# A raw-weight ring of six blocks, and four transfers for a paired chunk

## The chip, the core and the metric

The kernel runs on one core of a Trainium2 chip. Five engines work side by side, each through its own queue in order: TensorE (PE, matmuls; PEld is its loading of weights), VectorE (DVE), ScalarE (ACT), GpSimd (POOL) and SyncE (SP, which here only issues transfers). The metric is the device time of one execution in microseconds, lower is better. The profile is one execution taken by the hardware profiler.

## What is computed

One layer of a hybrid block over 512 latent tokens of width 1024, with 256 context tokens. From the normalised and modulated tokens `h`, one wide projection gives ten parts; two branches use them, a gated short convolution and an attention over neighbours, and their outputs are merged and projected.

```python
parts = _split_in(h @ w_in[i])                   # b, c, x, z_a, q, k, v, z_b, g_a, g_b
...
attn = _neighbourhood_attention(q, k, v, k_c, v_c, rpb[i])
...
y_a = (silu(z_a) * b_gate * _dwconv3(c_gate * x_in, conv_w, conv_b)) @ w_out_conv
y_b = (silu(z_b) * attn_o) @ w_out_attn
merged = sigmoid(g_a) * y_a + sigmoid(g_b) * y_b
y = merged @ w_o
x = x + gt[:, None, :] * _rmsnorm(y, post_g[i])
```

All of it is float32. The kernel reaches that precision by splitting every operand into a rounded high part H and a rest L (ACT casts H, DVE subtracts to get L) and multiplying H by H, H by L and L by H.

## The kernel before

**Weights come in chunks.** The host lays `w_in` and the two output projections out as chunks of 1024 rows by 256 columns, 1 MB each: two units of 128 columns side by side, in eight row blocks `k` of 128. `order` (L236 to L240) lists the chunks in the order of their use, and a `Chunks` object hands them out. A `Chunk` (L83) has two raw tiles `raw` of [128, 4, 256], one for the row blocks 0 to 3 and one for 4 to 7, and fills each with a transfer of 512 KB issued on SP (L89). The pool holds three such raw tiles; a fourth can be filled only when the first has no reader left.

**Two kinds of use.** A whole chunk goes through `split` (L91): for each raw tile one ACT cast (L67) and one DVE subtraction (L70) over 1024 elements a partition. A *paired* chunk (`paired`, L233: 20 of the 45) is multiplied by a block scheme with seven block products in place of eight. Its raw tiles are seen as four blocks: B11 and B12 are the two column halves of the first raw tile, B21 and B22 those of the second (L99). `first` (L98) splits B11 and B21 and the sums T1 = B11 + B12 (L102) and T2 = T1 + B22 (L105), adds B22 to B12 (L109) and T2 to B21 (L110), all in place. `second` (L114) splits what is left: T3 in the place of B12, T4 in that of B21, and B22. So the blocks of one raw tile end at different times: B11 with T2, in `first`, and B12 with T3, in `second`.

**Who waits for whom.** Each product runs on PE (`product`, L286; the matmuls are L289), in two halves of `pair` (L294): first B11, B21, T1 and T2, then T4, T3 and B22. L306 and L317 are DVE additions that free a PSUM bank for the next product, L314 further combinations. Between these products stand the attention's steps of the current pair of heads: scores (L721, L730), adding the relative bias and the row maximum on DVE (L737, from a tile `bt` loaded at L713), exponentials on ACT (L744, L748), scaling (L751), transposes on PE (L758), the split of the transposed block into `TH` and `TL` (L67, L70 again), and the product with the values (L777). Loop iterations interleave them by count (`step`, `fill`). While the attention runs, `Chunks.load` defers the first half of the splitting to the end of the iteration by way of the list `behind`.

**What sets the order.** Apart from a hand-written start, a scheduler places the instructions of each engine from their dependences, at build time. After that each engine takes its instructions in that order, and SP its transfers.

Chunk names below: qk*n* (queries and keys of pair *n*), gate chunk *n* (the gates of pairs 2*n* and 2*n*+1 in the attention branch), cx*n* and bz*n* (conv parts), v*n* (values).

Of the kernel before, what the change touches and what calls it, by code (L numbers as in the profile page):

```python
# [9 lines left out]
F32 = mybir.dt.float32  # L10
# [5 lines left out]
P = 128  # L16
D = 1024
KT = 8
S = 512
# [8 lines left out]
def layer(ctx: ExitStack, tc, xp, ctxt, ctxT, cc, wmod, small, wfirst, win, wout, wo, rel, tab, out):  # L28
    nc = tc.nc
# [3 lines left out]
    wp = ctx.enter_context(tc.tile_pool(name="wp", bufs=2))  # L33
# [4 lines left out]
    class Banks:  # L38


        def __init__(self, *tags):
            self.tags, self.n = tags, 0
# [21 lines left out]
    def split(H, L, src, scale=None, pinned=False):  # L64

        if scale is None:
            cast = nc.scalar.copy(H, src)  # L67
            if pinned:
                tc.keep_in_program_order(cast)
            nc.vector.tensor_sub(L, src, H.bitcast(F32))  # L70
        else:
            nc.scalar.mul(H, src, scale)
            nc.vector.scalar_tensor_tensor(
                out=L, in0=src, scalar=scale, in1=H.bitcast(F32), op0=ALU.mult, op1=ALU.subtract
            )
# [4 lines left out]
    def wtile(shape):  # L80
        return wp.tile(shape, F32R, name="w", bufs=4)

    class Chunk:  # L83


        def __init__(self, src):
            self.raws = [wp.tile([P, 4, 256], F32, name="raw", bufs=3) for _ in range(2)]
            for i, raw in enumerate(self.raws):
                nc.sync.dma_start(raw, src[:, 4 * i:4 * i + 4])  # L89

        def split(self):  # L91
            t = [wtile([P, 4, 2, 256]) for _ in range(2)]
            for x, raw in zip(t, self.raws):
                split(x[:, :, 0], x[:, :, 1], raw)
            k = range(KT)
            return tuple([t[i // 4][:, i % 4, y] for i in k] for y in range(2)) + ([t[i // 4][:, i % 4] for i in k],)

        def first(self, keep=False):  # L98
            (b11, b12), (b21, b22) = self.b = [(r[:, :, :P], r[:, :, P:]) for r in self.raws]  # L99
            t, sums = (wtile([P, 2, 2, 4, P]) for _ in range(2))  # L100
            split(t[:, 0, 0], t[:, 0, 1], b11)
            nc.vector.tensor_add(b11, b11, b12)  # L102
            split(sums[:, 0, 0], sums[:, 0, 1], b11)
            split(t[:, 1, 0], t[:, 1, 1], b21)
            nc.vector.tensor_add(b11, b11, b22)  # L105
            split(sums[:, 1, 0], sums[:, 1, 1], b11)
            self.keep = keep
            if not keep:
                nc.vector.tensor_add(b12, b12, b22)  # L109
            nc.vector.tensor_add(b21, b21, b11)  # L110
            self.B = {"B11": t[:, 0], "B21": t[:, 1], "T1": sums[:, 0], "T2": sums[:, 1]}
            return self
# [15 lines left out]
    class Chunks:  # L128
# [4 lines left out]

        def load(self, n):
            if n < len(self.srcs) and n not in self.ahead and n not in self.raw:
                self.raw[n] = Chunk(self.srcs[n][0])
                if behind is None:
                    self.ready(n)
                else:
                    behind.append(lambda: self.ready(n))  # L140
# [153 lines left out]
    def pair(c1, c2, w=None):  # L294

        w = w or chunk().B
        a, b, e = (pj()[:, :256] for _ in range(3))
        first, second = slice(0, 256), slice(256, S)
        product(a, A11, w["B11"], True)
        nc.scalar.copy(c1[:, first], a)  # L300
        product(b, A12, w["B21"], True)
        product(e, blocks_h["X1"], w["T1"], True)
        nc.scalar.copy(c2[:, second], e)
        product(a, blocks_h["S2"], w["T2"], False)
        nc.scalar.copy(c2[:, first], a)
        nc.vector.tensor_add(c1[:, first], c1[:, first], b)  # L306
        chunk.more()
        yield
        product(b, A22, w["T4"], True)
        product(a, blocks_h["S3"], w["T3"], False)  # L310
        nc.scalar.copy(c1[:, second], a)
        product(e, blocks_h["S4"], w["B22"], False)
        for cols, x in ((second, c1[:, second]), (first, e)):
            nc.vector.scalar_tensor_tensor(  # L314
                out=c2[:, cols], in0=c2[:, cols], scalar=-1.0, in1=x, op0=ALU.mult, op1=ALU.subtract
            )
        nc.vector.tensor_add(c1[:, second], c1[:, second], b)  # L317
# [35 lines left out]
    with ExitStack() as p0:  # L353
# [197 lines left out]
        w = chunk()  # L551
# [158 lines left out]
    def scores(p, h, b):  # L710
# [31 lines left out]
        if b % 2 == 0:  # L742
            z = aw.tile([P, 2], F32, name="z", bufs=4)
            nc.scalar.activation(pt, s, AF.Exp, bias=m, scale=-1.0, accum_out=z[:, 0:1])  # L744
            whole[:] = pt, z
        else:
            first, z = whole
            nc.scalar.activation(pt, s, AF.Exp, bias=m, scale=-1.0, accum_out=z[:, 1:2])  # L748
            nc.vector.reciprocal(z, z)  # L749
            for i, x in enumerate((first, pt)):  # L750
                nc.scalar.mul(x, x, z[:, i:i + 1])  # L751
# [96 lines left out]
    blocks = [(p, h, b) for p in range(NPAIR) for h in range(2) for b in range(4)]  # L848
# [54 lines left out]
    us, at = [], []  # L903
# [49 lines left out]
    for j in range(KT):  # L953
        w = chunk()
# [16 lines left out]
        if j == 4:  # L971
# [4 lines left out]
            for i in range(2):  # L976
                gb = cv.tile([P, S], F32, name="ta")
                ps = pj()
                for k in range(4):
                    n = 4 * i + k  # L980
# [3 lines left out]
        if j == 4:  # L984
            A11, S3 = operand("A11", hp, ("u2", "u3")), operand("S3", hp, ("a2", "a3"))
            for q in range(2):
                split(A11[q][:, 0], A11[q][:, 1], raws[q][:, :, h0])
                x = cv.tile([P, S], F32, name="tb").rearrange("p (k c) -> p k c", k=2)
# [219 lines left out]
```

## Time and profile before

| | |
|---|---|
| median of 3 runs | 708.86 us (708.29 to 710.21) |
| the profiled execution | 708.11 us, of which the profile spans 706.3 us |
| TensorE clock granted | 0.998 of full speed |
| DVE busy / ACT busy | 584.9 us / 437.1 us |
| transfers | 108.27 MB, mean 153 GB/s |
| raw halves from `w_in` | 74 transfers of 512 KB, 4.6 us to land (median) |
| raw halves from the output projections | 16 of 512 KB, 3.7 us |
| bias tiles `bt` | 16 of 256 KB, 2.8 us |

Busy time of PE is what the profile models from pipelined matmuls, whose ends lie beyond the next one's start. A bracket behind a row of a timeline is the idle time of that engine just before it and what ended it. In the transfers' rows, SPq is SP's queue, and a row that stands for several issues gives the time from the first to the last.

### The profile page before, as it was taken

How to read it: one execution, taken by the hardware profiler on the slowest of the kernel's cores; microseconds unless marked ns; L12 is line 12 of the kernel's file. 1: busy time of each engine (PE TensorE's matmuls, PEld its weight loads, DVE VectorE, ACT ScalarE, POOL GpSimd, SP SyncE). 2: the span in 40 equal slices, each digit the busy share in tenths (PEclk: the TensorE clock that was granted, in tenths of full speed). 3: DMA queues.
4: the chain of work that ended last, by engine and by line, in shares of the span. 5: the costliest groups of instructions: out<-in, count | busy, mean ns of one | idle time of the engine just before them, and what ended most of it. 6: DMA issues, size and time to landing. Idle time of an engine off the chain costs nothing.

```text
span 706.3 us, 11435 instructions
## 1 busy us (share of the span) xinstructions
PE 694.8 (98%) x4196; PEld 618.4 (88%) x4196; DVE 584.9 (83%) x1114; ACT 437.1 (62%) x868; POOL 67.3 (10%) x111
## 2 busy tenths in 40 slices
PE   7999999999999999999999999999999999999996
PEld 4888888888889989898999999999898899988885
DVE  6989996668599989978899697999799676665996
ACT  7676632556587677775886766878693444442563
POOL 0000003140130310301203103000000000000000
PEclk9999999999999999999999999999999999999999
DMA  9996885565351563552726336313733233570013
GB/s 353 406 344 241 306 329 147 131 170 144 91 109 29 133 177 109 126 137 66 169 101 182 89 122 154 105 61 107 249 115 116 86 120 120 184 264 30 31 59 120
DMA packets 37354, 108.27 MB, mean 153 GB/s; under 512 B 4897, under 2 KB 5153, under 8 KB 37298
## 3 DMA queue, kind: packets, MB, share of 16 engines
q1 hardware_dynamic: 28800, 92.16, 37.8%
q0 software_dynamic: 8352, 15.25, 10.9%
q8 instruction: 33, 0.54, 0.3%
q14 instruction: 23, 0.19, 0.1%
q10 hardware_dynamic: 146, 0.14, 0.1%
HBM read 87.07 MB, written 5.24 MB: 131 GB/s over the span
## 4 chain that ended last, share of the span: by engine, by line
PE 93%; DVE 3%; ACT 2%; DMA 1%; issue 0%; ACTq 0%; DVEq 0%; SPq 0%
PE ps L289 25%; PE ps L164 11%; PE ps L165 11%; PE ps L166 11%; PE ps L177 6%; PE ps L1012 5%; PE ps L777 4%; PE ps L758 4%; PE ps L182 3%; PE ps L721 3%; PE ps L196 2%; PE ps L424 2%; PE ps L430 2%; PE ps L427 2%; PE ps L201 1%; PE ps L730 1%
## 5 line engine op out<-in xcount | busy, mean ns | idle before, releaser
L70 DVE TENSOR_TENSOR w<-raw,w 128x512 fp32r<-128x512 f32 (+1 forms) x193 | 156.2, 823 | 40.0 <-ACT w L67 39.3
L67 ACT CAST w<-raw 128x512 fp32r<-128x512 f32 (+1 forms) x193 | 137.1, 732 | 81.9 <-PE ps L166 28.7
L289 PE MATMUL ps<-S,w 128*128 128x256 f32 x960 | 121.9, 283 | 0.0
L289 PEld LDWEIGHTS ps<-S,w 128*128 128x128 f32 x960 | 118.2, 192 | 0.1
L289 PE MATMUL ps<-h,w 128*128 128x256 f32 x720 | 94.0, 284 | 0.5 <-DVE tc L306 0.4
L289 PEld LDWEIGHTS ps<-h,w 128*128 128x128 f32 x720 | 89.9, 191 | 2.4 <-DVE tc L306 0.7
L164 PE MATMUL ps<-h,w 128*128 128x512 f32 x208 | 81.5, 392 | 0.0
L166 PE MATMUL ps<-h,w 128*128 128x512 f32 x208 | 81.2, 390 | 0.0
L165 PE MATMUL ps<-h,w 128*128 128x512 f32 x208 | 81.0, 389 | 0.0
L630 POOL DMA_DIRECT2D tc<-tb x32 | 28.5, 1165 | 284.1 <-DVE tc L628 197.1
L751 ACT ACTIVATE pt<-pt,z 128x512 f32<-128x512 f32 x64 | 43.0, 722 | 6.1 <-DVE z L749 5.9
L166 PEld LDWEIGHTS ps<-h,w 128*128 128x128 f32 x208 | 39.0, 188 | 8.3
L164 PEld LDWEIGHTS ps<-h,w 128*128 128x128 f32 x208 | 39.1, 188 | 7.9
L165 PEld LDWEIGHTS ps<-h,w 128*128 128x128 f32 x208 | 39.1, 188 | 8.0
L67 ACT CAST TH<-ps 128x512 fp32r<-128x512 f32 x64 | 35.8, 589 | 16.5 <-PE ps L758 16.3
L737 DVE CUSTOM_DVE_ANT_1 ps<-ps,bt 128x512 f32<-128x512 f32 x56 | 38.7, 692 | 7.5 <-PE ps L721 7.2
L70 DVE TENSOR_TENSOR TL<-ps,TH 128x512 fp32r<-128x512 f32 x64 | 42.2, 680 | 0.9 <-ACT TH L67 0.7
L758 PE MATMUL ps<-ident,pt 128*128 128x128 f32 x256 | 33.4, 273 | 0.0
L177 PE MATMUL ps<-w,h 128*128 128x512 f32 x128 | 32.3, 394 | 0.0
L758 PEld LDWEIGHTS ps<-ident,pt 128*128 128x128 f32 x256 | 29.2, 140 | 2.2 <-ACT pt L751 0.2
L744 ACT ACTIVATE pt<-ps,m 128x512 f32<-128x512 f32 x32 | 22.0, 689 | 12.6 <-DVE m L737 11.7
L777 PE MATMUL ps<-TH,V 128*128 128x256 f32 (+1 forms) x96 | 28.5, 319 | 0.2 <-ACT TH L67 0.2
(250 smaller groups left out, 1374.1 us busy)
## 6 DMA issues: line engine op xcount, KB each, us to landing
raw<-in_win SPq DMA_DIRECT2D x74, 512.0 KB, 4.6
wm<-in_wmod SPq DMA_DIRECT2D x34, 512.0 KB, 6.2
raw<-in_wout SPq DMA_DIRECT2D x16, 512.0 KB, 3.7
bt<-in_rel SPq DMA_DIRECT2D x16, 256.0 KB, 2.8
tc<-tb POOLq DMA_DIRECT2D x32, 128.0 KB, 3.4
B<-in_wo SPq DMA_DIRECT2D x8, 512.0 KB, 7.6
fraw<-in_wfirst SPq DMA_DIRECT2D x8, 384.0 KB, 8.3
qd<-qd POOLq DMA_DIRECT2D x24, 128.0 KB, 2.3
```

The costliest lines, as they stand in the source:

```text
L67: cast = nc.scalar.copy(H, src)
L70: nc.vector.tensor_sub(L, src, H.bitcast(F32))
L164: nc.tensor.matmul(ps, lhsT=H[k][:, cs], rhs=mH[k], start=k == 0, stop=False)
L165: nc.tensor.matmul(ps, lhsT=H[k][:, cs], rhs=mL[k], start=False, stop=False)
L166: nc.tensor.matmul(ps, lhsT=L[k][:, cs], rhs=mH[k], start=False, stop=k == KT - 1)
L177: nc.tensor.matmul(ps, lhsT=mH[k][:, ts], rhs=both[k].rearrange("p a c -> p (a c)"), start=k == 0, stop=False, skip_group_check=True,)
L289: nc.tensor.matmul(ps, lhsT=w[:, x, k], rhs=act[y][k], start=start and k + o == 0, stop=k == 3 and o == 2, skip_group_check=True,)
L737: nc.vector.tensor_tensor_reduce(out=s3, in0=s3, in1=bt[:, e::4 - e][:, 0:2], scale=-1.0, scalar=3.0e38, op0=ALU.add, op1=ALU.min, accum_o ...
L751: nc.scalar.mul(x, x, z[:, i:i + 1])
L758: nc.tensor.transpose(tp[:, c], pt[:, c * P:(c + 1) * P], ident)
L777: nc.tensor.matmul(o3[:, dst], lhsT=V[p][:, kt, h], rhs=src(t), start=n == 0 and t is TH, stop=n == len(work) - 1 and t is TL,)
L1012: nc.tensor.matmul(out, lhsT=a(x, k, ts), rhs=w[y][k // 2][:, k % 2, cols], start=start and k + o == 0, stop=k == 3 and o == 2, skip_group ...
```

## The change

The raw tiles give way to one tile, `ring`, of six blocks of 512 elements a partition, as large as the three raw tiles together. A chunk takes two turns of two blocks each, always the next two round the ring. The host now lays every chunk out by blocks: per partition, first the 4 x 128 elements of B11, then those of B12, B21 and B22. A whole chunk still comes in two transfers of 512 KB, now called two blocks each; a paired chunk comes in four of 256 KB, one a block. In `first` the four blocks are the ring's blocks themselves, and so contiguous; in `split` the two blocks of a half are read interleaved (row block, unit, column), so that H and L lie as they did. The number and size of the casts and subtractions is as before.

```diff
+    ring = wp.tile([P, 6, S], F32, name="ring", bufs=1)
+    turn = [0]
...
-        def __init__(self, src):
-            self.raws = [wp.tile([P, 4, 256], F32, name="raw", bufs=3) for _ in range(2)]
-            for i, raw in enumerate(self.raws):
-                nc.sync.dma_start(raw, src[:, 4 * i:4 * i + 4])
+        def __init__(self, src, blocks=False):
+            self.raws = []
+            for i in range(2):
+                at = 2 * (turn[0] % 3)
+                turn[0] += 1
+                for o, n in ((0, 1), (1, 1)) if blocks else ((0, 2),):
+                    nc.sync.dma_start(ring[:, at + o:at + o + n], src[:, 2 * i + o:2 * i + o + n])
+                self.raws.append(ring[:, at:at + 2].rearrange("p u (k c) -> p u k c", k=4))
...
             for x, raw in zip(t, self.raws):
-                split(x[:, :, 0], x[:, :, 1], raw)
+                H, L = (x[:, :, y].rearrange("p k (u c) -> p k u c", u=2) for y in range(2))
+                split(H, L, raw.rearrange("p u k c -> p k u c"))
...
         def first(self, keep=False):
-            (b11, b12), (b21, b22) = self.b = [(r[:, :, :P], r[:, :, P:]) for r in self.raws]
+            (b11, b12), (b21, b22) = self.b = [(r[:, 0], r[:, 1]) for r in self.raws]
...
-                self.raw[n] = Chunk(self.srcs[n][0])
+                self.raw[n] = Chunk(*self.srcs[n])
...
+    def by_block(w):
+        w = w.reshape(-1, 128, 2, 4, 2, 128).transpose(0, 1, 2, 4, 3, 5)
+        return np.ascontiguousarray(w).reshape(-1, 128, 4, 512)
+
+    win, wout = by_block(win), by_block(wout)
```

The scheduler places the instructions anew. The rows that follow stand in the programs as built; names carry buffer numbers, and the semaphores that an instruction waits for stand in brackets (DMAHW is one of eight counters that the transfers take in turn).

SP's queue, where cx5 is loaded. Before: raw_2314 is the second half of gate chunk 0, raw_2547 and raw_2548 are the halves of cx5, raw_2736 and raw_2737 those of qk4.

```order
L89 DMA raw_2314<-in_win 128x1024 [waits DMAHW6_49,DVE_49,Activation_49]
L89 DMA raw_2547<-in_win 128x1024 [waits DMAHW4_49,DVE_49]
L713 DMA bt_1039<-in_rel 128x512 [waits DMAHW1_49,DVE_49]
L89 DMA raw_2548<-in_win 128x1024 [waits DMAHW0_49,DVE_49,Activation_49]
L89 DMA raw_2736<-in_win 128x1024 [waits DMAHW3_49,DMAHW7_49,DVE_49,Activation_49]
L89 DMA raw_2737<-in_win 128x1024 [waits DMAHW4_49,DVE_49,Activation_49]
```

The change, same place: in this order B11 and B12 of cx5, B22 of gate chunk 0, B21 of cx5, the bias tile, B22 of cx5, and the four blocks of qk4.

```order
L96 DMA ring_104<-in_win 128x512 [waits DMAHW7_49,DVE_49,Activation_49]
L96 DMA ring_104<-in_win 128x512 [waits DMAHW0_49,DVE_49,Activation_49]
L96 DMA ring_104<-in_win 128x512 [waits DMAHW1_49,DVE_49]
L96 DMA ring_104<-in_win 128x512 [waits DMAHW2_49,DVE_49]
L722 DMA bt_1028<-in_rel 128x512 [waits DMAHW4_49,DMAHW3_49,DVE_49]
L96 DMA ring_104<-in_win 128x512 [waits DVE_49]
L96 DMA ring_104<-in_win 128x512 [waits DMAHW5_49,DVE_49,Activation_49]
L96 DMA ring_104<-in_win 128x512 [waits DMAHW1_49,DMAHW6_49,DVE_49,Activation_49]
L96 DMA ring_104<-in_win 128x512 [waits DMAHW7_49,DVE_49]
L96 DMA ring_104<-in_win 128x512 [waits DMAHW0_49,DVE_49]
```

The second half of cx5, one transfer behind the bias tile, has become two: B21 ahead of the bias tile, B22 behind it. B21 waits for the last split from B11 of gate chunk 0, B22 for the one from its B12, as the whole half did before.

DVE's order, where cx5's first operands are split. Before (w_2575 holds the splits of B11 and B21, w_2576 those of T1 and T2):

```order
L306 TENSOR_TENSOR tc_2482<-tc_2482,ps_2493 128x256 [waits PE_49]
L70 TENSOR_TENSOR w_2575<-raw_2547,w_2575 128x512 [waits DMAHW4_49,Activation_49]
L102 TENSOR_TENSOR raw_2547<-raw_2547 128x4x128 [waits DVE_49]
L737 ISA ps_2551,m_2554<-ps_2551,bt_1039 128x512 [waits PE_49]
L737 ISA m_2554 128x1
L70 TENSOR_TENSOR w_2575<-raw_2548,w_2575 128x512 [waits DMAHW6_49,Activation_49]
L70 TENSOR_TENSOR TL_2343<-ps_2561,TH_2342 128x512 [waits Activation_49]
L749 RECIPROCAL z_2470<-z_2470 128x2 [waits Activation_49]
L109 TENSOR_TENSOR raw_2547<-raw_2547,raw_2548 128x4x128 [waits DVE_49]
L70 TENSOR_TENSOR TL_2343<-ps_2562,TH_2342 128x512 [waits Activation_49]
L70 TENSOR_TENSOR w_2576<-raw_2547,w_2576 128x512 [waits Activation_49]
```

The change, same place (L315 is L306 of before, L111 is L102, L746 is L737, L118 is L109; w_2552 holds B11 and B21, w_2553 T1 and T2):

```order
L315 TENSOR_TENSOR tc_2459<-tc_2459,ps_2470 128x256 [waits PE_49,Activation_49]
L70 TENSOR_TENSOR w_2552<-ring_104,w_2552 128x512 [waits DMAHW7_49,Activation_49]
L70 TENSOR_TENSOR w_2552<-ring_104,w_2552 128x512 [waits DMAHW2_49,Activation_49]
L746 ISA ps_2528,m_2531<-ps_2528,bt_1028 128x512 [waits PE_49]
L746 ISA m_2531 128x1
L111 TENSOR_TENSOR ring_104<-ring_104 128x512 [waits DMAHW0_49,DVE_49]
L70 TENSOR_TENSOR TL_2320<-ps_2538,TH_2319 128x512 [waits Activation_49]
L70 TENSOR_TENSOR TL_2320<-ps_2539,TH_2319 128x512 [waits Activation_49]
L758 RECIPROCAL z_2447<-z_2447 128x2 [waits Activation_49]
L70 TENSOR_TENSOR w_2553<-ring_104,w_2553 128x512 [waits Activation_49]
L118 TENSOR_TENSOR ring_104<-ring_104 128x512 [waits DMAHW4_49]
```

The split of B21 has moved ahead of the first sum, and the first row that needs B22 (L118, waiting for its transfer) stands behind both TL. On ACT the cast of B21 has moved up in the same way, and the two casts of TH stand behind it and two copies of products.

DVE's order one gate chunk later, where cx6's first operands are split. Before (raw_3734 and raw_3735 are the halves of cx6):

```order
L70 TENSOR_TENSOR w_3767<-raw_3734,w_3767 128x512 [waits DMAHW5_49,Activation_49]
L102 TENSOR_TENSOR raw_3734<-raw_3734 128x4x128 [waits DVE_49]
L70 TENSOR_TENSOR w_3767<-raw_3735,w_3767 128x512 [waits DMAHW0_49,Activation_49]
L737 ISA ps_3743,m_3746<-ps_3743,bt_1039 128x512 [waits PE_49]
L737 ISA m_3746 128x1
L70 TENSOR_TENSOR w_3768<-raw_3734,w_3768 128x512 [waits Activation_49]
L70 TENSOR_TENSOR TL_3550<-ps_3753,TH_3549 128x512 [waits Activation_49]
L749 RECIPROCAL z_3667<-z_3667 128x2 [waits Activation_49]
L70 TENSOR_TENSOR TL_3550<-ps_3754,TH_3549 128x512 [waits PE_49]
```

The change, same place:

```order
L70 TENSOR_TENSOR w_3740<-ring_104,w_3740 128x512 [waits DMAHW1_49,Activation_49]
L70 TENSOR_TENSOR w_3740<-ring_104,w_3740 128x512 [waits DMAHW4_49,Activation_49]
L111 TENSOR_TENSOR ring_104<-ring_104 128x512 [waits DMAHW2_49,DVE_49]
L746 ISA ps_3716,m_3719<-ps_3716,bt_1028 128x512 [waits PE_49]
L746 ISA m_3719 128x1
L118 TENSOR_TENSOR ring_104<-ring_104 128x512 [waits DMAHW6_49,DVE_49]
L70 TENSOR_TENSOR TL_3523<-ps_3726,TH_3522 128x512 [waits Activation_49]
L758 RECIPROCAL z_3640<-z_3640 128x2 [waits Activation_49]
L70 TENSOR_TENSOR w_3741<-ring_104,w_3741 128x512
L70 TENSOR_TENSOR TL_3523<-ps_3727,TH_3522 128x512 [waits Activation_49]
```

Here the sum with B22 (L118, waiting for its transfer) has moved ahead of both TL; it stood behind them before.

## The prediction

> **What bounds the kernel now.** I read the page first, then the busy times in stretches of 20 us, then the chain of waits, and last the timeline of single engines around the one place where the first views show something.
>
> ```profile
> span 706.3 us, 11435 instructions
> ...
> PE 694.8 (98%) x4196; PEld 618.4 (88%) x4196; DVE 584.9 (83%) x1114; ACT 437.1 (62%) x868; POOL 67.3 (10%) x111
> ```
>
> ```profile
> 0.00:20.00 20.00, 15.76 (x56) 10.67 (x57) 14.60 (x33) 14.04 (x22) 1.41 (x7) 1.00 0.92 359
> ...
> 240.00:260.00 20.00, 19.39 (x152) 18.51 (x151) 17.51 (x37) 14.59 (x33) 7.18 (x11) 1.00 0.61 151
> 260.00:280.00 20.00, 19.47 (x153) 18.55 (x152) 18.91 (x41) 15.40 (x34) 1.02 (x2) 1.00 0.41 131
> ...
> 700.00:706.30 6.30, 0.18 (x2) 0.00 (x0) 2.88 (x8) 0.77 (x3) 0.00 (x0) 0.77 0.46 166
> sum 706.30, PE 694.79 PEld 618.35 DVE 584.85 ACT 437.11 POOL 67.29; mean PE 19.30 PEld 17.18 DVE 16.25 ACT 12.14 POOL 1.87
> ```
>
> The first figure behind a stretch's length is PE's busy time. PE is idle for 706.30 - 694.79 = 11.51 us. The start has 4.24 of it, the end 6.12, and the two stretches between 240 and 280 us have 0.61 and 0.53: these four make 11.50, so PE waits nowhere else. The weights of this change are not read in the first 20 us or the last 6, so only the middle can move. Now PE's own timeline there.
>
> ```profile
> 246.21 1.03 PE L758 MATMUL ps<-ident,pt 128*128 128x128 f32 x8
> 247.00 1.68 PE L289 MATMUL ps<-h,w 128*128 128x256 f32 x12
> 248.51 3.04 PE L289 MATMUL ps<-S,w 128*128 128x256 f32 x24
> 251.71 0.49 PE L777 MATMUL ps<-TH,V 128*128 128x512 f32 x1 [0.16 <-ACT TH L67]
> 252.66 0.50 PE L777 MATMUL ps<-TL,V 128*128 128x512 f32 x1 [0.45 <-DVE TL L70]
> 253.00 0.39 PE L777 MATMUL ps<-TH,V 128*128 128x512 f32 x1
> 253.23 0.39 PE L777 MATMUL ps<-TL,V 128*128 128x512 f32 x1
> ...
> 254.89 3.03 PE L289 MATMUL ps<-h,w 128*128 128x256 f32 x24
> 257.76 3.04 PE L289 MATMUL ps<-S,w 128*128 128x256 f32 x24
> ...
> 261.12 1.03 PE L758 MATMUL ps<-ident,pt 128*128 128x128 f32 x8
> 262.60 1.69 PE L289 MATMUL ps<-h,w 128*128 128x256 f32 x12 [0.44 <-DVE tc L306]
> ...
> 268.72 3.46 PE L289 MATMUL ps<-h,w 128*128 128x256 f32 x24
> 272.02 3.04 PE L289 MATMUL ps<-S,w 128*128 128x256 f32 x24
> ```
>
> A matmul's busy time runs past the start of the next, so a stall is measured from start to start. **Stall A:** 24 matmuls of 256 columns take 257.76 - 254.89 = 2.87 us where nothing is late, and 3.20 before 251.71: 0.33 too much. One of 512 columns takes 253.23 - 253.00 = 0.23, but 0.95 from 251.71 and 0.34 from 252.66: 0.72 and 0.11 too much. Together 1.16. **Stall B:** eight transposes take 0.79 from 246.21 to 247.00, but 1.48 before 262.60: 0.69. **Stall C:** 3.30 from 268.72 against 2.87: 0.43. The pool is 1.16 + 0.69 + 0.43 = 2.28 us, or 0.32% of the time. The Trainium skill ("Trainium Kernel Development and Optimization", Performance Expectations) calls matmul busy time a bad metric, because matmuls are pipelined. Read by busy time, the pool would be the 1.14 us of idle time and no more could be won than that; the starts show twice as much, so here the trace agrees with the page.
>
> What holds PE up there? The chain of waits has it in order:
>
> ```profile
> 243.56 5.82 DMA raw<-in_win
> 249.40 0.63 ACT w L67
> 250.05 0.69 DVE w L70
> ...
> 270.49 4.57 PE ps L289 x36
> ```
>
> ```profile
> 227.66 0.90 SPq L89 DMA_DIRECT2D raw<-in_win  x2
> ...
> 243.56 13.57 SPq L89 DMA_DIRECT2D raw<-in_win  x3
> ```
>
> ```profile
> 249.40 0.62 ACT L67 CAST w<-raw 128x512 fp32r<-128x512 f32 x1 [3.08 <-DMA raw<-in_win]
> 249.93 0.58 ACT L67 CAST TH<-ps 128x512 fp32r<-128x512 f32 x1
> ```
>
> ```profile
> 250.05 0.69 DVE L70 TENSOR_TENSOR w<-raw,w 128x512 fp32r<-128x512 f32 x1 [1.79 <-ACT w L67]
> ...
> 251.92 0.68 DVE L70 TENSOR_TENSOR TL<-ps,TH 128x512 fp32r<-128x512 f32 x1
> ...
> 266.94 0.69 DVE L70 TENSOR_TENSOR w<-raw,w 128x512 fp32r<-128x512 f32 x1 [0.72 <-ACT w L67]
> ```
>
> The transfer of 243.56 is the second half of conv chunk 5 (cx5). It could not start at 227.66 with the one ahead of it, because its buffer still held the first half of gate chunk 0, whose last block is split only at 243.5 us. It lands at 249.40. ACT stands 3.08 us and DVE 1.79 us at the split of its block B21, and behind it in both queues stand TH and TL, the operands of L777. That is stall A. From 250.05 on the chain to 270.49 is nearly all DVE, so B and C are DVE's lateness handed on to PE.
>
> **The change, part by part.** *Blocks that come free one by one.* In the ring, cx5's B21 takes the place of the gate chunk's B11, which is done with the last of that chunk's first four operands, rows ahead of its second four; only B22 has to wait for the split at 243.5. So the cast and the split of B21 find their data, and in the built program TH and TL stand behind nothing that comes late. The sum with B22 (b12 + b22) now stands behind both TL. That takes away ACT's 3.08 and DVE's 1.79 us. A goes whole: TH could start when its transposes end, at 247.1, and DVE has the two TL splits done by about 249.8 (six rows of 0.6 us from 246.2), 1.6 us before the 251.38 at which PE would ask for them. Since the chain from 250.05 to 270.49 runs on DVE, PE's start at 270.49 comes earlier by what DVE gains: **-1.79 us**. It cannot exceed the pool of 2.28, and it would reach it only if DVE's second wait, 0.72 at 266.94, also went. That wait is for an ACT cast that stood behind other ACT work, not behind a transfer, so I leave it. The lower end is A alone, -1.16, if DVE merely gets its work later for another reason.
>
> *The late block.* If B22 leaves at the same 243.5, when must it land? DVE's rows in the new order, from the end of L306's sum at 246.2 in the timeline of before: two splits, the bias row, one sum, two TL and one split, at about 0.6 us each, bring the sum with B22 up at about 250.4. It has 6.9 us. The nearest rows are the bias loads, which have the same 256 KB, and the halves of 512 KB:
>
> ```profile
> DMA to landing us min/median/max: 2.4/2.8/3.9
> ```
>
> ```profile
> DMA to landing us min/median/max: 3.1/4.5/10.2
> ```
>
> The first line is of the bias loads (L713), the second of the raw halves (L89). From both sides: 2.4 to 10.2 us. I take 4, near the bias loads, because the size is theirs; then nothing waits.
>
> *More transfers.* Twenty chunks are paired, and each has four transfers for two: 40 more. An issue takes SP some 0.3 to 0.45 us (two in 0.90 above), so 13 to 18 us of issue time, on an engine whose three issues from 243.56 fill 13.57 us with waiting. Cost 0. If that cover went, a bias load behind two more issues would come 0.9 us later.
>
> *Forms.* Paired operands become contiguous, and the splits of whole chunks read in runs of 128 elements where there were runs of 256 or more.
>
> ```profile
> L70 DVE TENSOR_TENSOR w<-raw,w 128x512 fp32r<-128x512 f32 x143 | 95.4, 684 | 16.1 <-ACT w L67 15.6
> L70 DVE TENSOR_TENSOR w<-raw,w 128x1024 fp32r<-128x1024 f32 x50 | 60.8, 1221 | 23.9 <-ACT w L67 23.7
> L70 DVE TENSOR_TENSOR V<-ta,V 128x128 fp32r<-128x128 f32 x48 | 11.7, 286 | 3.4 <-ACT V L67 3.3
> ```
>
> 512 more elements cost 1221 - 684 = 537 ns, 1.05 each. By that, 128 elements should take 684 - 384 x 1.05 = 281; V has them in runs of 64 and takes 286. So a run's start costs a few ns at most: 8 runs x 5 ns x 50 splits = 2 us of DVE at worst, -2 us if shorter strides helped, over stretches in which PE never waits. Cost on PE: 0.
>
> *Order.* The scheduler places the work anew. PE keeps its order except at two places of a dozen rows, DVE and ACT move by a few rows around the paired chunks. This is the part that I can bound least: the tightest place that I found is priced as the second rival.
>
> **Sum.** -1.79 + 0 + 0 + 0 = -1.79 us. The profiled execution took 708.11 us, with 706.3 of span, so it would be 706.32. The median of the runs shown is 708.86, 0.75 above that execution, and the changed kernel is measured as such a median: 708.86 - 1.79 = **707.1 us**.
>
> **Rivals.** *Handed on.* DVE works from 250 to 270 without a pause that a transfer explains, and whatever it gains is spent in its own backlog: stall A goes and B and C stay. For it speaks that DVE is 18.91 of 20 us busy from 260 on; against it, that PE needs no more from DVE than before. Gain 1.16: 707.7. *Slower, by a new transfer wait.* At the next such place, conv chunk 6 behind gate chunk 1, the new order has the sum with B22 ahead of both TL splits:
>
> ```profile
> 339.50 2.40 SPq L89 DMA_DIRECT2D raw<-in_win  x2
> ```
>
> ```profile
> 345.01 0.69 DVE L737 CUSTOM_DVE_ANT_1 ps<-ps,bt 128x512 f32<-128x512 f32 x1
> ```
>
> ```profile
> 349.26 0.40 PE L777 MATMUL ps<-TL,V 128*128 128x512 f32 x1
> ```
>
> B22 can leave at 339.50, when the old half left, and its sum comes up after the row of 345.01, at 345.6. From a late landing the second TL is 2.6 us away (sum, TL, a split, TL), and PE wants it at 349.26. So PE waits once the landing takes more than 349.26 - 2.6 - 339.50 = 7.2 us. At the longest landing of a raw half, 10.2, that is 3.0 us, and the same order stands at chunk 7: +6.0 - 1.79 = +4.2, or 713.1. Against it: the size is that of the bias loads, whose longest landing is 3.9. The Trainium skill ("DMA: Bandwidth & Descriptors", Bandwidth) advises batches of 1 MiB and more, against smaller ones as here; its fit in "Anatomy of one DMA" (2.0 us and bytes over 436 GB/s, for GpSimd's path) gives an estimate of 2.6 us for 256 KB. That is near the 2.8 measured and far below 7.2, so by the rule too this rival stays small. *It doesn't do what it says.* If the ring were guarded as one tile, every transfer would wait for all six blocks, and the halves would come no earlier. The waits in the built program differ from block to block, which speaks against it. No gain: 708.9.
>
> **How the numbers follow.** The forecast, a gain of 1.2 to 2.28, gets 0.66; handed on 0.20; no effect 0.07; slower 0.07. A measurement of this kernel can tell 0.3%, 2.13 us, from no change; that is 706.73. Only the upper part of my gain, together with runs as low as the profiled one, gets below it: 0.30 of the forecast's 0.66. So faster 0.30, within 0.3% 0.36 + 0.20 + 0.07 = 0.63, slower 0.07. The range begins at 708.11 - 2.28 = 705.8 and ends where the no-effect case lies with the scatter of the runs, 708.86 + 0.57 (the median over the lowest run, 708.29) = 709.4. That leaves the slower rival out.
>
> **What would show it.** Right: PE's busy time is full in 240 to 280; L777 there has no idle time ahead; the cast of cx5's B21 starts without a wait for a transfer; transfers of 256 KB land in about 3 us; PE's busy sum stays near 694.8 and the span is about 704.5. Wrong: idle PE time ahead of L777 near 349 us with DVE standing at the sum with B22 means the second rival; stalls still ahead of the matmuls that followed L306 and L317 mean the first; a wait of the size of the old one at cx5's B21 the third. If the first 20 us or the last 6 move by over 0.5 us, my reading of what the change touches was wrong.

## The result, and the profile after

The changed kernel takes **706.94 us** in the median of 22 runs (706.23 to 710.32); the kernel before, with it on the chip, 708.88 in 22 (706.96 to 710.90). The ratio is 0.9977, with a 95% interval of 0.9966 to 0.9988: 1.9 us less, at the edge of what can be told from no change. A second comparison, below, gave 0.9988 (0.9973 to 1.0002). In the two, three of 22 and five of 12 runs of the changed kernel lie at 709.6 to 710.4, at a granted clock of 0.995 to 0.996 in place of 0.997 to 0.999; without them its medians would be 706.84 and 707.00, and why they lie there no run shows. So the reading goes by the traces.

The busy times by stretches of the changed kernel; the first figure behind a stretch's length is PE's:

```profile
0.00:20.00 20.00, 15.38 (x49) 9.94 (x50) 13.48 (x31) 13.40 (x21) 1.42 (x7) 1.00 0.93 358
...
240.00:260.00 20.00, 19.72 (x157) 18.98 (x156) 19.56 (x44) 16.95 (x38) 7.44 (x12) 1.00 0.71 164
260.00:280.00 20.00, 20.00 (x162) 19.52 (x161) 18.16 (x38) 14.41 (x32) 0.79 (x2) 1.00 0.45 142
...
sum 705.60, PE 694.52 PEld 618.46 DVE 584.86 ACT 435.77 POOL 67.44; mean PE 115.75 PEld 103.08 DVE 97.48 ACT 72.63 POOL 11.24
```

The stretch from 260 on is now full, and that from 240 has 0.28 us of idle time where it had 0.61. PE's timeline shows which stalls went and which one came:

```profile
244.04 1.60 PE L298 MATMUL ps<-S,w 128*128 128x256 f32 x12
245.48 0.39 PE L730 MATMUL ps<-ks,qd 128*128 128x512 f32 x1
246.15 1.70 PE L298 MATMUL ps<-S,w 128*128 128x256 f32 x12 [0.28 <-ACT tc L309]
247.69 0.39 PE L730 MATMUL ps<-ks,qe 128*128 128x512 f32 x1
...
250.23 3.04 PE L298 MATMUL ps<-S,w 128*128 128x256 f32 x24
253.11 0.40 PE L786 MATMUL ps<-TH,V 128*128 128x512 f32 x1
253.34 0.40 PE L786 MATMUL ps<-TL,V 128*128 128x512 f32 x1
...
261.67 1.03 PE L767 MATMUL ps<-ident,pt 128*128 128x128 f32 x8
262.46 1.68 PE L298 MATMUL ps<-h,w 128*128 128x256 f32 x12
...
268.58 3.11 PE L298 MATMUL ps<-h,w 128*128 128x256 f32 x24
271.53 3.04 PE L298 MATMUL ps<-S,w 128*128 128x256 f32 x24
```

L786 (L777 before) starts with no idle time, and its next row 0.23 us later: **stall A is gone**. The transposes of 261.67 last 0.79 us to the next start: **B is gone**. The 24 matmuls of 268.58 take 2.95 us, where they took 3.30: **C is gone** too, but for 0.08. New is **stall D**: from 245.48 to 246.15 are 0.67 us where a matmul of 512 columns takes 0.23, and the twelve from 246.15 take 1.54 where the twelve from 244.04 take 1.44. That is 0.44 + 0.10, with rounding 0.55 us, and the row names what PE waits for, the copy of L309. Here is ACT:

```profile
243.85 0.39 ACT L67 CAST ks<-ta 128x256 fp32r<-128x256 f32 x1
244.15 0.68 ACT L753 ACTIVATE pt<-ps,m 128x512 f32<-128x512 f32 x1
244.73 0.19 ACT L753 ACTIVATION_READ_ACCUMULATOR pt<-ps,m 128x1 f32 x1
245.12 0.72 ACT L72 ACTIVATE qd<-tc 128x448 fp32r<-128x448 f32 x2 [0.20 <-DMA tc<-tb]
245.75 0.35 ACT L309 COPY tc<-ps 128x256 f32<-128x256 f32 x1
246.00 1.14 ACT L67 CAST w<-ring 128x512 fp32r<-128x512 f32 x2
```

The two casts of 246.00 are cx5's B11 and B21: no wait for a transfer, where B21 had 3.08 us of it. SP's queue shows why: B21 is the last of these four issues, and leaves at 238.0, where the half that held it left at 243.56 before.

```profile
227.04 11.27 SPq L96 DMA_DIRECT2D ring<-in_win  x4
```

But the copy of L309, which PE needs, now stands behind the ks cast (keys), an exponential and the two qd rows (the high part of the scaled queries). In the kernel before the same copy, L300 there, stood ahead of that cast:

```profile
241.77 0.36 ACT L300 COPY tc<-ps 128x256 f32<-128x256 f32 x1
242.02 0.41 ACT L67 CAST ks<-ta 128x256 fp32r<-128x256 f32 x1
```

For the comparisons below I sum all stalls of PE in a stretch: for each matmul the distance to the next start, less the usual one of its form (the medians over the program: 0.227 us for 512 columns, 0.120 for 256, 0.109 for 128). In 240 to 280 that gives 2.20 us before and 0.54 after. The second measure is the **middle**, from the first matmul on fH (the high part of the first weights) to the last matmul of all: 685.35 us before, 683.46 after, a gain of 1.89. It leaves out the start, which neither kernel changes and which still differed:

```profile
14.55 1.66 PE L424 MATMUL ps<-h,fH 128*128 128x512 f32 x6 [0.55 <-ACT h L522]
```

```profile
15.69 1.66 PE L433 MATMUL ps<-h,fH 128*128 128x512 f32 x6 [0.21 <-ACT h L531]
```

The first row is of the kernel before, the second of the changed one. That 1.14 us is why the profiled spans, 706.3 and 705.6, differ by 0.7 only.

### The profile page after: what moved, and what is told of

Same layout as the page of the kernel before. It is cut to its first block, busy times and chain, and to the rows that moved or that the text cites. A ratio compares the mean times of both kernels' runs of the same rounds, so it can differ in the third digit from the quotient of the medians.

```text
span 705.6 us, 11545 instructions
## 1 busy us (share of the span) xinstructions
PE 694.5 (98%) x4196; PEld 618.5 (88%) x4196; DVE 584.9 (83%) x1114; ACT 435.8 (62%) x868; POOL 67.4 (10%) x111
## 4 chain that ended last, share of the span: by engine, by line
PE 95%; DMA 2%; DVE 1%; SPq 1%; ACT 0%; issue 0%; POOL 0%; DVEq 0%; ACTq 0%
PE ps L298 28%; PE ps L174 11%; PE ps L173 11%; PE ps L175 11%; PE ps L186 6%; PE ps L1021 5%; PE ps L786 4%; PE ps L767 4%; PE ps L191 3%; PE ps L730 3%; PE ps L205 2%; PE ps L433 2%; PE ps L439 2%; PE ps L436 2%; DMA wm<-in_wmod 1%; PE ps L739 1%
## 5 line engine op out<-in xcount | busy, mean ns | idle before, releaser
L70 DVE TENSOR_TENSOR w<-ring,w 128x512 fp32r<-128x512 f32 (+1 forms) x193 | 156.2, 824 | 38.4 <-ACT w L67 37.9
L67 ACT CAST w<-ring 128x512 fp32r<-128x512 f32 (+1 forms) x193 | 135.7, 733 | 65.5 <-PE ps L175 20.6
L746 DVE CUSTOM_DVE_ANT_1 ps<-ps,bt 128x512 f32<-128x512 f32 x56 | 38.9, 694 | 8.5 <-PE ps L730 8.2
L786 PE MATMUL ps<-TH,V 128*128 128x256 f32 (+1 forms) x96 | 28.4, 318 | 0.0
```

The source lines that it names most:

```text
L746: nc.vector.tensor_tensor_reduce(out=s3, in0=s3, in1=bt[:, e::4 - e][:, 0:2], scale=-1.0, scalar=3.0e38, op0=ALU.add, op1=ALU.min, accum_o ...
L786: nc.tensor.matmul(o3[:, dst], lhsT=V[p][:, kt, h], rhs=src(t), start=n == 0 and t is TH, stop=n == len(work) - 1 and t is TL,)
```

## The experiments

Each ran with the kernel before on the same chip, and the ratio is to that; the kernel before had medians from 708.15 to 708.88 there. "Stalls" and "middle" are as above, from one profile each. Line numbers lie one or two higher where an edit adds lines.

| kernel | median us | ratio (95%) | stalls 240 to 280 | middle |
|---|---|---|---|---|
| before | 708.88 | | 2.20 | 685.35 |
| changed | 706.94 | 0.9977 (0.9966 to 0.9988) | 0.54 | 683.46 |
| two_transfers | 709.49 | 1.0010 (0.9996 to 1.0023) | 1.93 | 685.99 |
| late_block_first | 708.81 | 1.0008 (0.9996 to 1.0019) | 1.73 | 684.79 |
| late_block_again | 708.63 | 0.9998 (0.9986 to 1.0011) | 1.90 | 686.52 |
| cast_behind | 706.61 | 0.9973 (0.9962 to 0.9983) | 0.20 | 683.22 |
| copy_first | 706.40 | 0.9969 (0.9959 to 0.9979) | -0.02 | 682.91 |
| all_in_four | 707.10 | 0.9987 (0.9970 to 1.0005) | 0.52 | 683.75 |
| b22_twice | 707.76 | 0.9993 (0.9977 to 1.0009) | 1.89 | 685.46 |

### The ring without the four transfers

```diff
-                for o, n in ((0, 1), (1, 1)) if blocks else ((0, 2),):
+                for o, n in ((0, 2),):
```

> The ring and the block layout as in the changed kernel, but every chunk comes in two transfers of 512 KB. My theory: the gain came from the transfer of B21 alone, which leaves without waiting for the block that is split last. Then the cast of conv chunk 5's B21 again waits 2 to 3 us for a transfer that starts near 243.5 us, the stalls of PE between 240 and 280 us add up to 1.8 to 2.8 us (start to start), and the time is that of the kernel before (ratio 0.999 to 1.001). Rival, layout or a new order of rows: the stalls there stay at or below 0.6 us, as in the changed kernel, and the ratio is near 0.998.

ACT, DVE and PE of this kernel at cx5:

```profile
249.78 0.62 ACT L67 CAST w<-ring 128x512 fp32r<-128x512 f32 x1 [2.80 <-DMA ring<-in_win]
250.30 0.58 ACT L67 CAST TH<-ps 128x512 fp32r<-128x512 f32 x1
```

```profile
250.43 0.69 DVE L70 TENSOR_TENSOR w<-ring,w 128x512 fp32r<-128x512 f32 x1 [1.68 <-ACT w L67]
```

```profile
253.04 0.50 PE L786 MATMUL ps<-TL,V 128*128 128x512 f32 x1 [0.45 <-DVE TL L70]
...
262.98 1.69 PE L298 MATMUL ps<-h,w 128*128 128x256 f32 x12 [0.48 <-DVE tc L315]
```

ACT waits 2.80 us, DVE 1.68, and PE stalls at the same two rows as before; C is there too (0.25 us at 270.87). So ring and layout alone give nothing: the stalls of 1.93 lie in the range of the theory and far from the rival's 0.6. The middle is even 0.6 us longer than before, since at 500.64 another wait for a transfer (2.34 us of ACT at 497.28) reaches PE.

### A smaller transfer that starts late

The scheduler sorts the transfers by what is ready first; here the second half's two are bound so that B22 goes ahead.

```diff
-                for o, n in ((0, 1), (1, 1)) if blocks else ((0, 2),):
-                    nc.sync.dma_start(ring[:, at + o:at + o + n], src[:, 2 * i + o:2 * i + o + n])
+                for o, n in ((i, 1), (1 - i, 1)) if blocks else ((0, 2),):
+                    load = nc.sync.dma_start(ring[:, at + o:at + o + n], src[:, 2 * i + o:2 * i + o + n])
+                    if blocks and i and o == 0:
+                        tc.keep_in_program_order(load)
```

> Four transfers as in the changed kernel, but of the second half the late block, B22, is sent ahead of B21, so that B21 leaves only behind the wait at 243.5 us. The order of ACT's rows at conv chunk 5 becomes that of the two-transfer kernel. If an early start is what matters: stall A comes back, 0.5 us or more ahead of L777's matmul (line numbers move by 2). If a transfer of half the size is enough: B21 lands 3 to 4.5 us after 243.9, by about 248, 1.4 us or more earlier than in the kernel before, ACT waits under 2 us and stall A is below 0.2 us; with the copy of L309 ahead of the qd rows there (it would cost 0.55 us otherwise) the sum of the stalls in 240 to 280 is then below that of the changed kernel.

ACT and PE:

```profile
246.06 0.72 ACT L72 ACTIVATE qd<-tc 128x448 fp32r<-128x448 f32 x2 [2.24 <-DMA tc<-tb]
...
248.34 0.62 ACT L67 CAST w<-ring 128x512 fp32r<-128x512 f32 x1 [0.18 <-DMA ring<-in_win]
```

```profile
248.42 1.70 PE L300 MATMUL ps<-h,w 128*128 128x256 f32 x12 [0.52 <-DVE tc L317]
...
252.83 0.40 PE L788 MATMUL ps<-TH,V 128*128 128x512 f32 x1
```

Neither theory fits. B21 was there by 248.34 and L788 did not stall, yet the sum of the stalls was 1.73: ACT had stood 2.24 us for another transfer, tc<-tb (issued by POOL, for the rotary embedding of the queries), and the lateness of DVE went on to PE at 248.42, at B and at C. One profile could not say whether that was chance, so the kernel ran again.

> The kernel of late_block_first a second time, for one question: there B21 landed in time for L788's matmul, but ACT stood 2.24 us at the qd rows for the tc<-tb transfer that took 4.66 us, and the stall moved to 248.42. If that landing was chance, the wait is now below 1 us as in the other kernels (0.2 to 0.8), the stall of 0.69 at 248.42 is gone, and the stalls in 240 to 280 are below 1 us. If the two transfers of 256 KB that leave at 244.2 hold it up, the wait is over 1.5 us again and the stalls are near 1.7 us.

ACT in the second profile:

```profile
244.85 0.72 ACT L72 ACTIVATE qd<-tc 128x448 fp32r<-128x448 f32 x2 [0.88 <-DMA tc<-tb]
...
249.43 0.62 ACT L67 CAST w<-ring 128x512 fp32r<-128x512 f32 x1 [2.48 <-DMA ring<-in_win]
```

The wait for tc<-tb was 0.88, so its length changes from one execution of a program to the next. But with ACT on time, B21 came too late: it landed at 249.43, and stall A stood there again (0.72 us at 252.69, B and C behind it). So neither expectation for it holds as written: the wait was short, and the stalls were 1.90 by way of the other one. The smaller size gains nothing that can be relied on: counted from the issue of the first of the two, at 244.1 to 244.2, B21 was there after 4.1 us in one profile and 5.3 in the other, where the half of 512 KB takes 5.2 to 6.0 (four profiles). What the changed kernel's gain rests on is that B21 leaves early.

The middle of the second profile is 1.2 us longer than that of the kernel before, though the stalls at cx5 are not. The same pattern stands once more further on: ACT waits for a weight block, DVE's split of that block and the second TL come late behind it, and PE stalls, 1.6 us in all between 485 and 489.

```profile
483.61 0.62 ACT L67 CAST w<-ring 128x512 fp32r<-128x512 f32 x1 [1.38 <-DMA ring<-in_win]
```

```profile
488.06 0.50 PE L788 MATMUL ps<-TL,V 128*128 128x512 f32 x1 [0.91 <-DVE TL L70]
```

### The same transfers as before, one cast bound

If the harm is done by what stands behind the waiting cast, then moving that cast must help without any ring. This is the kernel before with one argument added, in `first`; `pinned` binds the cast to its place in the program, here behind the cast of T1:

```diff
-            split(t[:, 1, 0], t[:, 1, 1], b21)
+            split(t[:, 1, 0], t[:, 1, 1], b21, pinned=True)
```

> The kernel before with its three buffers and its transfers as they were; only ACT's cast of B21 of every paired chunk is bound behind the cast of T1, so that at conv chunk 5 both TH casts stand ahead of it, while the transfer still lands near 249.4 us. My theory, that stall A is not the late transfer itself but what is queued behind the instruction that waits for it: ACT's wait of 3.08 us and DVE's of 1.79 us shrink to under 1.2 us each, stall A falls below 0.3 us, and the stalls of PE in 240 to 280 add up to 0.3 to 1.3 us in place of 2.28; ratio about 0.998 to 0.999. Rival, only an early transfer helps: PE waits as long, now ahead of the matmul on B21 or of the sums after it, the stalls stay at 2 us or more and the ratio is 1.000 or above.

ACT, DVE and PE:

```profile
247.51 1.07 ACT L67 CAST TH<-ps 128x512 fp32r<-128x512 f32 x2 [0.52 <-PE ps L758]
...
249.68 1.13 ACT L67 CAST w<-raw 128x512 fp32r<-128x512 f32 x2
```

```profile
248.83 1.28 DVE L70 TENSOR_TENSOR TL<-ps,TH 128x512 fp32r<-128x512 f32 x2
```

```profile
252.06 0.40 PE L777 MATMUL ps<-TH,V 128*128 128x512 f32 x1
252.29 0.40 PE L777 MATMUL ps<-TL,V 128*128 128x512 f32 x1
...
261.41 1.67 PE L289 MATMUL ps<-h,w 128*128 128x256 f32 x12
...
267.52 3.32 PE L289 MATMUL ps<-h,w 128*128 128x256 f32 x24
```

Buffers and transfers are as before, and yet ACT waits for no weights here: both TH casts run at 247.51, 2.8 us earlier than with two_transfers, and when the casts of T1 and B21 come up at 249.68 the data are there. They landed at 249.37, so there is little to spare: in the second profile of this kernel, below, they landed at 250.38 and DVE waited 0.25 us for them. A and B are gone, and the ratio is 0.9973. The stalls are 0.20 us, under my 0.3 to 1.3, and all of that is at C's place, the 24 matmuls of 267.52; in the second profile C is 0.35, as before the change. The rival falls: no early transfer was needed. The Trainium skill ("PSUM — Partial Sum Buffer", Engine vs sequencer instructions) calls the queues of ScalarE and VectorE strict FIFO; these rows agree: what is gained is that two ready casts, 1.07 us of work, are no longer queued behind a wait.

### The new stall, taken away

For gate chunk 0 the copy of L309 gets priority in the scheduler (`early` is true for that chunk alone). In the built program this one row of ACT moves ahead of five others, and one matmul of PE moves behind twelve.

```diff
-        nc.scalar.copy(c1[:, first], a)
+        with tc.high_priority() if early else nullcontext():
+            nc.scalar.copy(c1[:, first], a)
```

> The changed kernel with one row of ACT moved: the copy of L309 for gate chunk 0 stands ahead of one pt row, the ks cast and the two qd rows, where it stands behind them in the changed kernel. My theory: these rows cost PE the stall of 0.55 us at 246.15, which goes; nothing else changes, and the time is 0.5 us below the changed kernel's (ratio about 0.997 of before). Rival: ACT's backlog only moves the stall to a later row, the qd rows or the TH casts: the sum of stalls in 240 to 260 stays near 0.55.

ACT and PE:

```profile
242.10 0.35 ACT L310 COPY tc<-ps 128x256 f32<-128x256 f32 x1
242.35 0.73 ACT L761 ACTIVATE pt<-pt,z 128x512 f32<-128x512 f32 x1
```

```profile
242.91 3.04 PE L298 MATMUL ps<-S,w 128*128 128x256 f32 x24
245.79 0.40 PE L731 MATMUL ps<-ks,qd 128*128 128x512 f32 x1
246.02 0.39 PE L731 MATMUL ps<-ks,qe 128*128 128x512 f32 x1
```

The 24 matmuls run through and nothing stalls to 280. The middle is 682.91, 0.55 us below the changed kernel, just the size of D.

### More small transfers, and a late block made later

All 45 chunks in four transfers:

```diff
-                for o, n in ((0, 1), (1, 1)) if blocks else ((0, 2),):
+                for o, n in ((0, 1), (1, 1)):
```

> The changed kernel with every chunk in four transfers, 50 more of them. If issues on SP and smaller transfers cost nothing, as I priced them: the PE stalls outside the first 20 us stay within 0.3 us of the changed kernel's, and the time within 0.1%. Rival: the issues delay the loads of w_mod and the bias tiles, or the smaller transfers are slower; then PE waits at the whole chunks between 14 and 200 us, 0.2 us or more at each of several, and the time is 1 us or more above the changed kernel's.

Fifty more transfers cost 0.29 us in the middle, all of it one stall at 519.32 (0.19 ahead of that row and 0.10 behind it); the whole chunks between 14 and 200 us show no new one. The median is 0.16 us above the changed kernel's, within the 0.1%.

For the late block's slack, B22 of the paired cx chunks is sent twice to the same place; the rows around cx5 stay where they were.

```diff
-                    nc.sync.dma_start(ring[:, at + o:at + o + n], src[:, 2 * i + o:2 * i + o + n])
+                    for _ in range(2 if blocks == "cx" and i and o else 1):
+                        nc.sync.dma_start(ring[:, at + o:at + o + n], src[:, 2 * i + o:2 * i + o + n])
```

> The changed kernel, with block B22 of the paired conv and gate chunks of kind cx sent twice to the same place, so that it is there one landing later; the rows of DVE, ACT and PE around conv chunk 5 stay as they are. My estimate of the late block's slack says: B22 leaves at 244.1, one landing of such a block took 4.5 to 5.9 us there, so the second is in place at 253 to 256; DVE comes to the sum with it (L118) at 251.5 and waits 1.6 to 4.5 us for a transfer; the sum of L315 that PE needs at 262.5 was ready 0.9 us early, so PE stalls there by the wait less 0.9, 0.7 to 3.6 us, and the wait is handed on as in the kernel before. Rival, DVE has more slack than I think or the block lands sooner: no wait of DVE for a transfer over 0.5 us at L118 and no PE stall in 250 to 270 over 0.3 us.

SP's queue, DVE, ACT and PE (the sum is L119 here):

```profile
243.04 13.81 SPq L97 DMA_DIRECT2D ring<-in_win  x6
```

```profile
249.73 0.69 DVE L70 TENSOR_TENSOR w<-ring,w 128x512 fp32r<-128x512 f32 x1 [0.16 <-ACT w L67]
252.40 0.69 DVE L119 TENSOR_TENSOR ring<-ring 128x512 f32<-128x512 f32 x1 [1.98 <-DMA ring<-in_win]
```

```profile
253.13 2.27 ACT L67 CAST w<-ring 128x512 fp32r<-128x512 f32 x4 [1.93 <-DVE ring L119]
```

```profile
259.31 1.69 PE L299 MATMUL ps<-S,w 128*128 128x256 f32 x12 [0.24 <-ACT tc L310]
```

DVE waits 1.98 us, inside the 1.6 to 4.5. It stands there from 252.40 - 1.98 = 250.42 on, so B22, sent at 243.04, has 7.4 us before anyone waits. PE loses 1.35 us more in 240 to 280 than in the changed kernel, but not where I said: not 0.7 us or more at the matmul behind L316's sum, but mostly in pieces of 0.16 to 0.40 from 255.95 to 270.26, since four of ACT's casts stand behind the same sum. Its middle is 2.0 us longer than the changed kernel's: 0.6 us more of stalls stand at 487.88, where neither ACT nor DVE waits for a transfer, and no run follows that up.

### Side by side

The changed kernel and the two others that gained, on one chip.

> The changed kernel, on one chip with the next two, for the order of the three. By the middle of their traces (first fH matmul to last matmul) it needs 683.46 us where the kernel before needs 685.35: ratio 0.9973, or about 1.9 us less.

> The kernel of copy_first. By its middle, 682.91, 0.55 us below the changed kernel: ratio near 0.9966. Rival: the 0.55 us is chance of one profile, and both medians agree within 0.2 us.

> The kernel of cast_behind: three buffers and two transfers for every chunk, only one cast bound. By its middle, 683.22, 0.24 us below the changed kernel: ratio near 0.9970. Rival: the ring gives something beyond the order, and this kernel is 0.5 us or more above the changed one.

| kernel | median us | ratio (95%) | stalls 240 to 280 | middle |
|---|---|---|---|---|
| changed | 707.82 | 0.9988 (0.9973 to 1.0002) | 0.61 | 683.59 |
| copy_first | 706.28 | 0.9959 (0.9941 to 0.9976) | -0.01 | 683.03 |
| cast_behind | 706.71 | 0.9968 (0.9954 to 0.9981) | 0.38 | 683.29 |

The middles repeat to 0.13 us and keep their order: copy_first 0.56 and cast_behind 0.30 below the changed kernel. The medians have the same order, but lie further apart than the traces explain, 1.54 us between copy_first and the changed kernel; why stays open. The ratio expected for it, 0.9973, lies at the interval's end. copy_first is the fastest version found, 2.3 and 2.6 us below the kernel before in the two comparisons. That it beats the changed kernel too rests on the traces, by 0.55 us or 0.08%; on this chip its six runs (to 706.60) also lie just below the lowest of the changed kernel's twelve (706.62).

## Why the prediction was right, step by step

The prediction, 707.1, lies 0.2 us from the median, and 0.2% is within the 0.3% that held most of its chance. Of its steps:

- **What bounds the kernel, and stall A.** Right. A was a wait for cx5's second half, handed on through the queues of ACT and DVE: two_transfers brings the wait back and A with it, and cast_behind removes A without touching the transfer. One reading was too wide: by busy time I said that PE waits nowhere else, but from start to start 0.28 us of stalls stand between 480 and 520 as well. The changed kernel has 0.02 there; no run shows why.
- **B and C are DVE's lateness.** Right for B, and for C in part. All three go together in the changed kernel, copy_first and all_in_four, and in late_block_first B and C stood without A, as soon as DVE was late for another reason. So the rival *handed on*, by which B and C would stay, is out. But in cast_behind A and B go and C stays, at 0.20 and 0.35 us.
- **The term of -1.79 us.** The mechanism was right, the size was not. The whole pool came back, 2.20 us by the sums, where I took 1.79 because DVE's second wait of 0.72 would remain. It did remain, as the changed kernel's row shows, and C went all the same. C waits for a sum on DVE (L317 before). Counted from the first fH matmul, that sum ends at 255.9 us before, at 254.0 in cast_behind, where C partly stays, and at 253.5 in copy_first, where it goes. A wait that I did not count makes 0.35 of the 0.54 us between the last two: DVE stands 0.48 us for the qd rows in the kernel before and 0.52 in cast_behind, but 0.17 in copy_first. In the changed kernel the sum ends at 254.0 as well, and C goes because PE itself comes 0.45 us later than in cast_behind, behind stall D.

```profile
244.57 0.76 DVE L73 SCALAR_TENSOR_TENSOR qe<-tc,qd 128x448 fp32r<-128x448 f32 x2 [0.48 <-ACT qd L72]
```

```profile
266.20 0.69 DVE L70 TENSOR_TENSOR w<-ring,w 128x512 fp32r<-128x512 f32 x1 [0.72 <-ACT w L67]
```

- **Order, priced at 0.** The step that failed. I called it the part that I could bound least and looked only at places behind the late block; the new order cost 0.55 us elsewhere, at a copy that PE waits for. copy_first shows it. The two errors nearly cancel: with the 0.26 us that the stalls lose between 480 and 520, -2.20 - 0.26 + 0.55 = -1.91, against -1.89 measured in the middle and -1.79 forecast. That the forecast came so close is luck to that extent: without stall D the gain was 2.44 us, as the middle of copy_first shows.
- **The late block.** Nothing waited for it, as forecast. I took 4 us for its landing and expected some 3 in the trace; the median of all 80 blocks is 2.9, but the three sent between 244.1 and 245.7, which were under way together, took more:

```profile
DMA to landing us min/median/max: 4.5/4.8/5.9
```

In copy_first the three took 6.1 to 6.8 us. The slack of 6.9 us was measured as 7.4, so 0.6 us was left at the longest of these landings, and no more than that. The estimate of 2.6 us from the Trainium skill ("DMA: Bandwidth & Descriptors", Anatomy of one DMA) is near the median of all blocks but too small here by 1.9 to 3.3 us; its fit is for GpSimd's path, and whether the path or the other transfers under way make the difference no run shows. By it the slower rival looked safer than it was; b22_twice shows that it is a real mechanism, 1.35 us for one more landing.
- **More transfers and forms, priced at 0.** Right within what can be seen: 0.29 us for fifty more, and DVE is busy 584.86 us where it was 584.85.
- **What would show it.** Two signs were set too tight. Only one of the two stretches became full, because of D. And a start that moved by over 0.5 us was to mean that I had misread what the change touches; it moved by 1.14, but over all these profiles, the kernel before among them, the first fH matmul starts anywhere from 14.55 to 15.69 us with the same program ahead of it (14.55 and 15.26 in the two profiles of copy_first). For the same reason the span is 705.6 us and not 704.5.

## What to carry to other kernels

Where an engine takes its work in order, the price of a late transfer is the ready work queued behind the one instruction that waits for it; look there first, since moving that one instruction a few rows back gave here what a new buffer scheme gave. When a change makes a scheduler place the work anew, look on every engine for the copies that the bounding engine waits for, not only near the change. And compare small gains between two marks inside the trace that lie clear of the start.

## What the runs showed that was not expected

Two transfers of 256 KB sent one behind the other were not much quicker than one of 512 KB: the second landed 4.1 and 5.3 us after the first was issued, the single one after 5.2 to 6.0 (before, two_transfers, and cast_behind twice). And one small transfer between tiles, tc<-tb, kept ACT waiting for 0.88 us in one profile and 2.24 in another of the same kernel, which was enough to bring 1.7 us of stalls into the second.
